# Merge gates of a hybrid encoder layer, computed two at a time as a block product of seven products in place of eight

## The chip, the cores and the metric

The kernel runs on one core of one Trainium2 chip. The metric is the time of the program on the device in microseconds. TensorE (PE) multiplies, its weight loads (PEld) run beside it; VectorE (DVE), ScalarE (ACT) and GpSimd (POOL) do the rest; SyncE (SP) issues DMAs.

## The reference, cut to what matters

Two layers. In each, x of 512 tokens by 1024 channels is projected once by w_in; the columns feed latent attention (branch A), differential attention (branch B) and the merge gates. All is float32.

```python
h = x @ w_in[l]
c_q, c_kv, k_r, gate_a, q_d, k_d, v_d, gate_b, gates = _split_cols(h)
...
y_a = o_a.transpose(0, 2, 1, 3).reshape(b, s, MLA_WIDTH) * jax.nn.silu(gate_a)
y_a = y_a @ w_branch_a[l]
...
y_b = o_b.transpose(0, 2, 1, 3).reshape(b, s, DIFF_WIDTH) * jax.nn.silu(gate_b)
y_b = y_b @ w_branch_b[l]
g = jax.nn.sigmoid(gates + b_merge[l])
merged = g[..., :D_MODEL] * y_a + g[..., D_MODEL:] * y_b
out = merged @ w_out[l]
x = _layer_norm(DEEPNORM_ALPHA * x + out, ln_gamma[l], ln_beta[l])
```

The gates are 2048 columns of w_in, sixteen blocks of 128 channels: eight for branch A (A0 to A7), eight for branch B.

## The kernel before, in words

**Number format.** Each float32 operand is held as two tiles, a rounded high part (written by ACT, a cast) and the rest (DVE, a subtraction), and each product is three matmuls: high by high, high by rest, rest by high (`mm3`, L123 to L126). x lies transposed in xH and xL, channels on the partitions in eight blocks (k), tokens along the free dimension.

**Weights.** `slot` (L107) loads a block of 128x1024 into a raw tile of tag wr (two buffers), casts it whole on ACT into a tile wh (L110), and subtracts in two halves on DVE into wl (L113); wh and wl have three buffers each. `proj` (L128) multiplies such a block with all of x: eight k by three matmuls of 128x512 into one bank of PSUM (tag acc, three buffers).

**Gates.** `gate` (L506) is one `proj` of block gtA c or gtB c and one tanh on ACT (L510); the sigmoid is (tanh + 1) / 2. `mergeA` (L514) multiplies it with the branch's product and keeps the result in SBUF (tag vs) until branch B's is added (L600, L601). `branch` (L496) multiplies the branch's output with w_branch, two blocks of 128 columns from one loaded slot (brA0 to brA3, brB0 to brB3).

**Order of work in a layer.** Latent projections; eight latent heads, of which the scores of one are woven with the values of the last; four differential heads, woven the same way; between them the lists `fill` and `dfill` put projections: g is a gate of branch A, m its merge, b, q, k, v are gate B, key, query and value projections. Branch B's gates and branches follow, then w_out and the normalisation. A scheduler then sets each engine's order from the program; each engine works in that order, and an instruction waits on the semaphores of what it reads or overwrites. A buffer of a tag is taken again in turn when its last reader is done. All loads are issued by SP, in one queue.

**Softmax.** `soft` (L167) takes a maximum on DVE and an exponential on ACT (L172) for each block of 128 queries; `keyT` (L175) transposes on PE and splits on ACT and DVE (L181, L182). `diff_k` (L411 on) splits a rotated key into four tiles: six casts on ACT (L413 to L420), two subtractions on DVE (L415, L416) after the rotation (L394 to L398).

GpSimd has only small powers (L236, L485, L645).

Of the kernel before, what the change touches and what calls it, by code (L numbers as in the profile page):

```python
# [50 lines left out]
def hybrid_trunk(ctx: ExitStack, tc: tile.TileContext, x, xT, wlat, wts, prm, dlam, gb, tab, rtab, out):  # L51
# [70 lines left out]

    def mm3(o, lh, ll, rh, rl, start, stop):  # L123
# [61 lines left out]
    def layer(l, last):  # L185
        pr = prms[:, l, :]
# [36 lines left out]
        for t in range(NT):  # L223
# [12 lines left out]
            nc.gpsimd.tensor_tensor(ss, ss, mhalf[:, 0:2], ALU.pow)  # L236
# [222 lines left out]
        def diff_values(h, pts, v, g, s1):  # L459
# [30 lines left out]
            yB.append(split(o, "lat"))  # L490
# [5 lines left out]
        def branch(which, c, ys):  # L496
# [3 lines left out]
            acc = pt_("acc")  # L500
# [5 lines left out]
        def gate(which, c):  # L506
            acc = proj(l, f"gt{'AB'[which]}{c}")
            th = t2("tmp")
            col = which * 8 + c
            nc.scalar.activation(th, acc, AF.Tanh, bias=bh[:, col:col + 1], scale=0.5)  # L510
# [27 lines left out]
        def run(names):  # L538
            for f in names:
# [3 lines left out]
                elif f[0] == "g":  # L543
                    hold[i] = gate(0, i)
# [238 lines left out]
```

## Time and profile before

| what | us |
|---|---|
| median of three runs (lowest, highest) | 858.61 (858.48, 859.12) |
| the profiled execution | 860.1 |
| its span in the trace | 858.3 |
| PE busy in it | 843.5 |
| DVE, ACT, POOL busy | 588.7, 429.0, 21.8 |
| bytes read from HBM, written | 70.80 MB, 4.19 MB |

A group's row reads: line, engine, operation, tile written <- tiles read, shapes, count; then busy us in all and mean ns of one; then how long the engine stood idle just before these and who ended it. A row of the timeline reads: start in us, length in us, engine, line, operation. Matmuls overlap each other, so their spacing is read from their starts. The granted clock of PE was 0.998 over the span.

### The profile page before, as it was taken

The page shows a single profiled execution, that of the slowest core. Times are in us where ns is not written, and L with a number is a line of the kernel's source. Part 1 is how long each engine was busy: PE and PEld are TensorE (multiplying, and loading weights), DVE is VectorE, ACT ScalarE, POOL GpSimd, SP SyncE. Part 2 cuts the span into 40 slices and gives each one's busy share as a digit, 9 for nine tenths or more (in the row PEclk, how much of TensorE's full clock was granted, in tenths as well). Part 3 has the DMA queues.
Part 4 walks back from the last instruction along what each step waited for, and adds up shares of the span by engine and source line. Part 5 has one row for each costly group of instructions (what it writes and reads, how often), then busy time and mean ns, then how long its engine had stood idle before and what let it go on. Part 6 is the DMA issues. An engine that isn't in the chain of part 4 may idle for free.

```text
span 858.3 us, 11026 instructions
## 1 busy us (share of the span) xinstructions
PE 843.5 (98%) x4121; PEld 693.1 (81%) x4121; DVE 588.7 (69%) x1066; ACT 429.0 (50%) x843; POOL 21.8 (3%) x30
## 2 busy tenths in 40 slices
PE   9899999999999999999999999999999999999996
PEld 7678778878888888888897878788788888888885
DVE  6789998686646745455857899876667466545457
ACT  5767786463534633332236776755546354433310
POOL 0100000000000000000110000000000000000001
PEclk9999999999999999999999999999999999999999
DMA  8310111213222352233514010112222223432322
GB/s 294 124 44 31 38 56 55 74 31 100 92 74 74 122 178 82 93 97 118 183 43 139 17 37 26 50 50 74 75 74 74 76 97 123 152 98 95 99 74 98
DMA packets 27701, 75.70 MB, mean 88 GB/s; under 512 B 3200, under 2 KB 7808, under 8 KB 27648
## 3 DMA queue, kind: packets, MB, share of 16 engines
q1 hardware_dynamic: 27648, 75.01, 27.4%
q8 instruction: 32, 0.52, 0.2%
q14 instruction: 21, 0.17, 0.1%
HBM read 70.80 MB, written 4.19 MB: 87 GB/s over the span
## 4 chain that ended last, share of the span: by engine, by line
PE 87%; ACT 5%; DVE 4%; DMA 2%; issue 1%; POOL 0%; SPq 0%; DVEq 0%; ACTq 0%
PE psacc L124 22%; PE psacc L126 22%; PE psacc L125 22%; PE pstr L179 4%; PE pspv L366 2%; PE pssc L124 2%; PE pspv L124 2%; PE pssc L126 2%; PE pssc L125 2%; PE pspv L367 1%; PE pspv L125 1%; PE pspv L126 1%; DMA wr<-in_wts_dram 1%; ACT wh L110 1%; PE pssc L445 1%; PE pssc L450 1%
## 5 line engine op out<-in xcount | busy, mean ns | idle before, releaser
L113 DVE TENSOR_TENSOR wl<-wr,wh 128x512 fp32r<-128x512 f32 x192 | 127.0, 687 | 149.4 <-ACT wh L110 149.0
L124 PE MATMUL psacc<-xH,wh 128*128 128x512 f32 x512 | 203.6, 398 | 0.0
L126 PE MATMUL psacc<-xH,wl 128*128 128x512 f32 x512 | 202.5, 395 | 0.0
L125 PE MATMUL psacc<-xL,wh 128*128 128x512 f32 x512 | 201.1, 393 | 0.0
L110 ACT CAST wh<-wr 128x1024 fp32r<-128x1024 f32 x96 | 100.6, 1049 | 177.2 <-PE psacc L125 111.8
L126 PEld LDWEIGHTS psacc<-xH,wl 128*128 128x128 f32 x512 | 96.4, 188 | 20.9
L125 PEld LDWEIGHTS psacc<-xL,wh 128*128 128x128 f32 x512 | 96.3, 188 | 20.4
L124 PEld LDWEIGHTS psacc<-xH,wh 128*128 128x128 f32 x512 | 96.4, 188 | 19.5
L172 ACT ACTIVATE p<-pssc,sm 128x512 f32<-128x512 f32 x128 | 88.1, 690 | 25.2 <-DVE sm L170 24.5
L170 DVE TENSOR_REDUCE sm<-pssc 128x1 f32<-128x512 f32 x128 | 86.8, 684 | 4.5 <-PE pssc L126 1.9
L182 DVE TENSOR_TENSOR pt<-pstr,pt 128x512 fp32r<-128x512 f32 x96 | 65.0, 686 | 8.4 <-ACT pt L181 7.8
L181 ACT CAST pt<-pstr 128x512 fp32r<-128x512 f32 x96 | 55.6, 586 | 27.7 <-PE pstr L179 27.2
L179 PE MATMUL pstr<-ident,p 128*128 128x128 f32 x384 | 57.3, 272 | 0.0
L179 PEld LDWEIGHTS pstr<-ident,p 128*128 128x128 f32 x384 | 47.4, 140 | 12.0 <-ACT p L172 0.5
L124 PE MATMUL psacc<-wh,xH 128*128 128x256 f32 (+1 forms) x164 | 48.8, 297 | 0.0
L125 PE MATMUL psacc<-wl,xH 128*128 128x256 f32 (+1 forms) x164 | 48.6, 296 | 0.1
L126 PE MATMUL psacc<-wh,xL 128*128 128x256 f32 (+1 forms) x164 | 48.0, 294 | 0.0
L125 PEld LDWEIGHTS psacc<-wl,xH 128*128 128x128 f32 x164 | 31.0, 189 | 1.2 <-DVE wl L203 0.8
L124 PEld LDWEIGHTS psacc<-wh,xH 128*128 128x128 f32 x164 | 30.8, 188 | 0.8 <-ACT xH L120 0.5
L126 PEld LDWEIGHTS psacc<-wh,xL 128*128 128x128 f32 x164 | 30.8, 188 | 0.2
L366 PE MATMUL pspv<-pt,vs 128*128 128x512 f32 x64 | 29.2, 456 | 0.6 <-ACT pt L181 0.3
L124 PE MATMUL pssc<-kv,qm 128*128 128x512 f32 x64 | 26.7, 422 | 0.4 <-ACT kv L323 0.2
(233 smaller groups left out, 1502.5 us busy)
## 6 DMA issues: line engine op xcount, KB each, us to landing
wr<-in_wts_dram SPq DMA_DIRECT2D x106, 512.0 KB, 3.6
p<-in_xT_dram SPq DMA_DIRECT2D x8, 256.0 KB, 5.2
qr<-in_wts_dram SPq DMA_DIRECT2D x16, 128.0 KB, 2.1
p<-in_gb_dram SPq DMA_DIRECT2D x8, 256.0 KB, 3.0
y<-in_x_dram SPq DMA_DIRECT2D x8, 256.0 KB, 4.8
x_scratch<-y SPq DMA_DIRECT2D x8, 256.0 KB, 2.1
y<-x_scratch SPq DMA_DIRECT2D x8, 256.0 KB, 5.2
out_dram<-y SPq DMA_DIRECT2D x8, 256.0 KB, 2.0
```

The lines of the kernel that those rows point to most:

```text
L110: nc.scalar.copy(hi, raw)
L113: nc.vector.tensor_tensor(lo[:, c], raw[:, c], fr(hi[:, c]), ALU.subtract)
L124: nc.tensor.matmul(o, lhsT=lh, rhs=rh, start=start, stop=False)
L125: nc.tensor.matmul(o, lhsT=lh, rhs=rl, start=False, stop=False)
L126: nc.tensor.matmul(o, lhsT=ll, rhs=rh, start=False, stop=stop)
L170: nc.vector.tensor_reduce(m, S, axis=AX.X, op=ALU.max, negate=True)
L172: nc.scalar.activation(p, S, AF.Exp, bias=m, scale=1.0, accum_out=sums)
L179: nc.tensor.transpose(b[:, t * P:(t + 1) * P], pts[t][:, c * P:(c + 1) * P], ident)
L181: nc.scalar.copy(h, b)
L182: nc.vector.tensor_tensor(lo, b, fr(h), ALU.subtract)
L366: nc.tensor.matmul(pv, lhsT=v, rhs=ph, start=kc == 0, stop=False)
L367: nc.tensor.matmul(pv, lhsT=v, rhs=pl, start=False, stop=kc == NT - 1)
```

## The change

**The scheme.** Two neighbouring gate blocks c and c + 1 are now one product. The weights are cut in four: rows by channel half (x blocks 0 to 3, or 4 to 7), columns by gate, called r11, r12, r21, r22 in the code; x is cut by channel half and by token half (256 tokens). Each quarter product is four k by three matmuls of 128x256. Seven are made in place of eight. Their weight sides are W11, W12, W22 and the sums F1, F2, F3, F4 of the raw quarters, made by four adds on POOL and each split on ACT and DVE like any weight (`form`); their x sides are blocks of xH and xL and four sums of x, `XF`.

**Sums of x.** `x_forms` makes them on POOL at the layer's start, behind the last small power there, 24 adds and subtractions, and stores them to DRAM by 8 DMAs that POOL issues. `load_x_form` loads them back by SP through tag wr behind the latent heads (x0, x1) and behind the first gate B projection (x2, x3), and splits them.

**Where the sums of products go.** Products share three banks: Y, Z and X, of tag acc. Y takes W11's, then is copied out and goes on accumulating F2's, F3's and W22's; Z takes F1's and F4's; X takes W12's. Copies and sums (on ACT and DVE, 256 columns each) give the two gates t0 and t1.

**Room.** Branch A's raw quarters take both buffers of tag wr; branch B's take four tiles of tag p. A pair takes four of the wh and wl buffers in turn: W11 and F1; F2 and F4; F3 and W12; W22. Branch B's products with w_branch go into tag sc.

**Branch A's half.** It is no longer kept in SBUF but stored to DRAM (`mAd`) and loaded back for branch B, both issued by POOL. yB's halves and the last two merged tiles take other tags. The packing puts two neighbouring gates' columns side by side; the time of that is not in the metric.

```diff
+        def x_forms(j):
+            ra, rb, f, g = (t2("y") for _ in range(4))
+            for r, k in ((ra, j), (rb, j + 4)):
+                nc.gpsimd.tensor_tensor(r, fr(xH[:, k, :]), fr(xL[:, k, :]), ALU.add)
+            c1, c2 = slice(0, 256), slice(256, 512)
+            nc.gpsimd.tensor_tensor(f[:, c1], ra[:, c1], ra[:, c2], ALU.subtract)
...
+            for i, v in ((0, f), (2, g)):
+                nc.gpsimd.dma_start(xf[:, i:i + 2, j * 256:(j + 1) * 256], v.rearrange("p (a b) -> p a b", a=2))
+        with tc.issue_after(last_pow.ins):
+            for j in range(4):
+                x_forms(j)
...
-            yB.append(split(o, "lat"))
+            yB.append(split(o, "qm" if h < 2 else "y"))
...
-            acc = pt_("acc")
+            acc = pt_("sc" if which else "acc")
...
-        def gate(which, c):
-            acc = proj(l, f"gt{'AB'[which]}{c}")
-            th = t2("tmp")
+        def gate_pair(which, c):
+            G = gates_of(l, which)[c // 2]
...
+            def form(raw, rm, half):
+                hi, lo = (v[:, half * 512:half * 512 + 512] for v in rm)
+                nc.scalar.copy(hi, raw)
+                nc.vector.tensor_tensor(lo, raw, fr(hi), ALU.subtract)
+                return hi, lo
+            def add(o, a, b):
+                nc.gpsimd.tensor_tensor(o, a, b, ALU.add)
+            r11, r12, r21, r22 = r
+            s1 = room()
+            W11 = form(r11, s1, 0)
+            add(r11, r11, r21)
+            add(r21, r21, r22)
+            F1 = form(r21, s1, 1)
+            add(r21, r11, r22)
+            s2, s3 = room(), room()
+            F2 = form(r21, s2, 0)
+            W12 = form(r12, s3, 1)
+            add(r12, r12, r21)
+            F4 = form(r12, s2, 1)
+            F3 = form(r11, s3, 0)
+            W22 = form(r22, room(), 0)
...
+            def product(o, w, xs_, first):
+                for k in range(4):
+                    (wh, wl), (h, lo) = (v[:, k * P:(k + 1) * P] for v in w), xs_[k]
+                    for n, (a, b) in enumerate(((wh, h), (wl, h), (wh, lo))):
+                        nc.tensor.matmul(o, lhsT=a, rhs=b, start=first and k == 0 and n == 0,
+                                         stop=k == 3 and n == 2, skip_group_check=True)
...
+            product(Y, W11, block(0, 0), True)
+            nc.scalar.copy(t0[:, c1], Y)
+            product(Z, F1, xform(0), True)
+            nc.scalar.copy(t1[:, c1], Z)
+            product(Y, F2, xform(1), False)
+            nc.scalar.copy(t0[:, c2], Y)
+            product(Z, F4, block(1, 1), False)
+            nc.vector.tensor_tensor(t0[:, c2], Z, t0[:, c2], ALU.add)
+            product(Y, F3, xform(2), False)
+            nc.scalar.copy(t1[:, c2], Y)
+            product(X, W12, block(1, 0), True)
...
+            product(Y, W22, xform(3), False)
...
-            m = mA[-1][:, (c % 2) * 512:(c % 2) * 512 + 512]
-            nc.vector.scalar_tensor_tensor(m, th, 1.0, acc, ALU.add, ALU.mult)
+            nc.vector.scalar_tensor_tensor(th, th, 1.0, acc, ALU.add, ALU.mult)
+            nc.gpsimd.dma_start(mAd[:, c * 512:(c + 1) * 512], th)
...
-        run(["b0", "v0"])
+        run(["b0", "x2", "x3", "v0"])
...
-            0: ["g0", "m0", "g1", "m1", "b1", "q2", "k2", "g2", "m2", "g3", "m3"],
-            1: ["v1", "b2", "q3", "k3", "g4", "m4", "g5", "m5"],
-            2: ["b3", "g6", "m6", "g7", "m7"],
+            0: ["b1", "p0", "m0", "m1", "q2", "k2", "p2", "m2", "m3"],
+            1: ["v1", "b2", "q3", "k3", "p4", "m4", "m5"],
+            2: ["b3", "p6", "m6", "m7"],
...
+                m = t2("kv")
+                nc.gpsimd.dma_start(m, mAd[:, c * 512:(c + 1) * 512])
```

**What stands where, first place: PE in layer 0, where head 2's scores follow branch A's second pair of blocks.** Before, the last matmuls of the branch (psacc_2315), then the scores of the key (qm_2213 to qm_2216), then transposes of head 1:

```order
L124 MATMUL psacc_2315<-y_1614,wh_2261 128x512
L125 MATMUL psacc_2315<-y_1615,wh_2261 128x512
L126 MATMUL psacc_2315<-y_1614,wl_2262 128x512
L445 MATMUL pssc_2330<-qm_2213,qm_2169 128x512
L446 MATMUL pssc_2330<-qm_2215,qm_2169 128x512
L449 MATMUL pssc_2337<-qm_2214,qm_2170 128x512
L450 MATMUL pssc_2337<-qm_2216,qm_2170 128x512
L179 MATMUL pstr_2349<-ident,p_1857 128x128
```

After, the last two matmuls of X (psacc_2395), the scores of the key (qm_2349 to qm_2352), then Z (psacc_2394, form F4 in wh_2374) and Y (psacc_2393, form F3 in wh_2376) by turns:

```order
L594 MATMUL psacc_2395<-xH,wl_2377 128x256
L594 MATMUL psacc_2395<-xL,wh_2376 128x256
L475 MATMUL pssc_2528<-qm_2349,qm_2305 128x512
L479 MATMUL pssc_2535<-qm_2350,qm_2306 128x512
L190 MATMUL pstr_2547<-ident,p_2031 128x128
L476 MATMUL pssc_2528<-qm_2351,qm_2305 128x512
L190 MATMUL pstr_2556<-ident,p_2031 128x128
L480 MATMUL pssc_2535<-qm_2352,qm_2306 128x512
L594 MATMUL psacc_2394<-xH,wh_2374 128x256
L594 MATMUL psacc_2393<-vs_1718,wh_2376 128x256
L594 MATMUL psacc_2393<-vs_1718,wl_2377 128x256
L594 MATMUL psacc_2394<-xH,wl_2375 128x256
```

Before, two gates and two branches stood between the key's projection and its scores; now the first four products of the pair stand there, and the scores stand inside the pair. The first matmuls of the branch (of weights wh_2492) stand now ahead of the pair's last product.

**Second place: ACT at the same point.** Before, behind the cast of gate A3's weights (wh_2283), the six casts of the key, then the tanh of gate A2:

```order
L110 CAST wh_2283<-wr_2281 128x1024
L413 CAST qm_2213<-tmp_2210 64x512
L414 CAST qm_2214<-tmp_2210 64x512
L418 CAST qm_2213<-qm_2213 64x512
L418 CAST qm_2215<-qm_2215 64x512
L420 CAST qm_2214<-qm_2214 64x512
L420 CAST qm_2216<-qm_2216 64x512
L510 ACTIVATE tmp_2257<-psacc_2232,bh_326 128x512
```

After, the key's six casts (L443 to L450), then form F4's (wh_2374), the copies of Z and Y, head 2's first exponentials, and the cast of the branch's weights (wh_2492), whose raw tile wr_2490 takes the buffer of wr_2361:

```order
L444 CAST qm_2350<-tmp_2346 64x512
L448 CAST qm_2349<-qm_2349 64x512
L450 CAST qm_2350<-qm_2350 64x512
L448 CAST qm_2351<-qm_2351 64x512
L450 CAST qm_2352<-qm_2352 64x512
L561 CAST wh_2374<-wr_2361 128x512
L604 COPY qw_2392<-psacc_2394 128x256
L606 COPY qw_2391<-psacc_2393 128x256
L183 ACTIVATE p_2533,s_469_1850<-pssc_2528,sm_2531 128x512
L192 CAST pt_2552<-pstr_2547 128x512
L183 ACTIVATE p_2540,sm_2527<-pssc_2535,sm_2538 128x512
L111 CAST wh_2492<-wr_2490 128x1024
```

F4's cast and the copies of the pair stand behind the key's casts, and the branch's cast behind them all.

**Third place: ACT in branch B, layer 0, third pair.** Before, casts of whole slots (L110), tanh (L510) and the split of merged tiles (L163):

```order
L110 CAST wh_3438<-wr_3436 128x1024
L510 ACTIVATE tmp_3355<-psacc_3330,bh_326 128x512
L110 CAST wh_3472<-wr_3470 128x1024
L510 ACTIVATE tmp_3389<-psacc_3364,bh_326 128x512
L163 ACTIVATE qm_3413<-tmp_3355 128x512
L110 CAST wh_3506<-wr_3504 128x1024
L163 ACTIVATE qm_3432<-tmp_3389 128x512
```

After, W12 and F3 (wh_3919), the copy of Y, F4 (wh_3917 from p_3901), a merged tile (qm_3896), W22 (wh_3930), the copies of Z and Y, the branch's weights (wh_4037):

```order
L561 CAST wh_3919<-p_3901 128x512
L561 CAST wh_3919<-p_3900 128x512
L602 COPY qw_3934<-psacc_3936 128x256
L561 CAST wh_3917<-p_3901 128x512
L174 ACTIVATE qm_3896<-tmp_3753 128x512
L561 CAST wh_3930<-p_3905 128x512
L604 COPY qw_3935<-psacc_3937 128x256
L606 COPY qw_3934<-psacc_3936 128x256
L111 CAST wh_4037<-wr_4035 128x1024
```

The copy of Z, which Z's second product waits for, stands behind F4's cast, a merged tile's and W22's.

More of the change, by code (lines that the diff above doesn't have):

```diff
@@ L39 @@
     + ["qd0", "kd0", "ga1", "qd1", "kd1", "ga2", "ga3"]
[3 rows of a table removed]
+    + ["vd00", "vd01", "gb0", "brA0", "gb1", "qd2", "kd2", "brA1"]
+    + ["vd10", "vd11", "gb2", "qd3", "kd3", "brA2", "gb3", "brA3"]
+    + ["brB0", "brB1", "brB2", "brB3"]
+    + [f"gt{w}{c}" for w in "AB" for c in range(8)]
     + [f"o{n}{k}" for n in range(2) for k in range(4)]
@@ L121, in load_x, with gates_of @@
         nc.vector.tensor_tensor(xL[:, k, :], raw, fr(xH[:, k, :]), ALU.subtract)
+    def gates_of(l, which):
+        i = SLOTS.index(f"gt{'AB'[which]}0")
+        return wts[l, i:i + 8].rearrange("(c s) (q r) n -> c (s q) (r n)", s=2, r=2)
     def mm3(o, lh, ll, rh, rl, start, stop):
@@ L185, in layer @@
     def layer(l, last):
+        xf = dram.tile([P, 4, 1024], F32, name=f"xf{l}")
+        mAd = dram.tile([P, 8 * 512], F32, name=f"mA{l}")
         pr = prms[:, l, :]
@@ L235, in layer @@
             nc.vector.tensor_scalar(ss[:, 1:2], ss[:, 1:2], 1.0 / 256, EPS_RMS, ALU.mult, ALU.add)
-            nc.gpsimd.tensor_tensor(ss, ss, mhalf[:, 0:2], ALU.pow)
+            last_pow = nc.gpsimd.tensor_tensor(ss, ss, mhalf[:, 0:2], ALU.pow)
             nc.vector.tensor_copy(kr[:, t, :], acc[:, 384:416])
@@ L542, in run @@
                     gateA(i)
-                elif f[0] == "g":
-                    hold[i] = gate(0, i)
+                elif f[0] == "p":
+                    hold[i], hold[i + 1] = gate_pair(0, i)
+                elif f[0] == "x":
+                    load_x_form(i)
                 elif f[0] == "m":
@@ L590, in layer @@
             run(dfill[h])
-        hold["B0"] = gate(1, 0)
+        ths = gate_pair(1, 0)
         next(tail)
@@ L594, in layer @@
         for c2 in range(4):
-            ths = [gate(1, 2 * c2) if c2 else hold.pop("B0"), gate(1, 2 * c2 + 1)]
+            if c2:
+                ths = gate_pair(1, 2 * c2)
             for i in range(2):
                 c = 2 * c2 + i
+                m = t2("kv")
+                nc.gpsimd.dma_start(m, mAd[:, c * 512:(c + 1) * 512])
                 acc = branch(1, c, yB)
@@ L600, in layer @@
                 nc.vector.scalar_tensor_tensor(th, th, 1.0, acc, ALU.add, ALU.mult)
-                nc.vector.tensor_tensor(th, th, mA[c // 2][:, i * 512:i * 512 + 512], ALU.add)
-                merged.append(split(th, "qm", 0.5))
+                nc.vector.tensor_tensor(th, th, m, ALU.add)
+                merged.append(split(th, "qm" if c < 6 else "pt", 0.5))
         src = x if l == 0 else xs
@@ L696, in _pack @@
         c = int(s[-1]) if s[-1].isdigit() else 0
+        if s.startswith("gt"):
+            if c % 2:
+                continue
+            o = O_GT + (DM if s[2] == "B" else 0) + c * P
+            a = np.concatenate([_fm(w_in, o + r(P)).reshape(P, DM), _fm(w_in, o + P + r(P)).reshape(P, DM)], 1)
+            outs += list(a.reshape(2, P, 1024))
+            continue
         if s.startswith("vd"):
@@ L701, in _pack @@
             a = _fm(w_in, o + c * P + r(P))
-        elif s.startswith("gt"):
-            a = _fm(w_in, O_GT + (DM if s[2] == "B" else 0) + c * P + r(P))
         elif s.startswith("qup"):
```

40 lines of the change are left out of this document (34 added, 6 removed), and 3 rows, old and new, of the table SLOTS.

## The prediction

> **What bounds the kernel now.** I read the page's first part, then the table of stretches over layer 0, then the groups by shape, then two timelines. The engine totals:
>
> ```profile
> PE 843.5 (98%) x4121; PEld 693.1 (81%) x4121; DVE 588.7 (69%) x1066; ACT 429.0 (50%) x843; POOL 21.8 (3%) x30
> ```
>
> The stretches of layer 0 in which the change acts (the columns are length, then busy time of PE, PEld, DVE, ACT and POOL, each with its instructions, then the granted clock, the DMA share and GB/s); they hold the differential heads with branch A's gates (172 to 300), and the last head and branch B (300 to 386):
>
> ```profile
> 172.00:300.00 128.00, 128.00 (x633) 105.76 (x632) 85.71 (x166) 65.14 (x139) 3.02 (x3) 1.00 0.26 82
> 300.00:327.00 27.00, 26.95 (x132) 21.77 (x131) 13.46 (x22) 10.65 (x22) 1.01 (x1) 1.00 0.45 148
> 327.00:386.00 59.00, 59.00 (x259) 48.41 (x258) 29.63 (x46) 20.73 (x26) 0.00 (x0) 1.00 0.31 97
> ```
>
> PE works 213.95 of these 214 us at full clock. So fewer PE cycles are worth their whole price here, and every wait that the change brings is paid in full as well: nothing is there to absorb it.
>
> **What the products take off PE.** Matmuls overlap, so their price is the step from one start to the next, not the duration in the third column. From PE's timeline, the first and last of 50 matmuls of 256 columns and of 67 of 512:
>
> ```profile
> 239.80 0.28 PE L125 MATMUL psacc<-wl,xH 128*128 128x256 f32 x1
> ...
> 245.57 0.28 PE L126 MATMUL psacc<-wh,xL 128*128 128x256 f32 x1
> 245.69 0.40 PE L124 MATMUL psacc<-xH,wh 128*128 128x512 f32 x1
> ...
> 261.09 0.40 PE L124 MATMUL psacc<-xH,wh 128*128 128x512 f32 x1
> ```
>
> 49 steps in 5.77 us are 0.118 us each; 66 steps in 15.40 us are 0.233. Half the columns cost half the time, weight loads included (they hide behind the matmuls in both). Before, 32 gates of 24 matmuls are 768 x 0.2333 = 179.2 us; after, 16 pairs of 84 are 1344 x 0.1178 = 158.3. That is 20.9 us less, 10.4 a layer, 1.3 a pair. One product is 12 x 0.118 = 1.41 us, a pair 9.9.
>
> **What must now be ready inside a pair.** A gate before had one cast, made long ahead, and one chain of 24 matmuls. A pair has seven forms, each an ACT cast and a DVE subtraction, four POOL adds between them, and copies of Y and Z that must be read out before PE goes on accumulating. The durations, from the groups:
>
> ```profile
> L113 DVE TENSOR_TENSOR wl<-wr,wh 128x512 fp32r<-128x512 f32 x192 | 127.0, 687 | 149.4 <-ACT wh L110 149.0
> L110 ACT CAST wh<-wr 128x1024 fp32r<-128x1024 f32 x96 | 100.6, 1049 | 177.2 <-PE psacc L125 111.8 <-issue 27.5 <-PE psacc L126 21.3
> L160 ACT CAST qm<-tmp 128x512 fp32r<-128x512 f32 x16 | 9.9, 619 | 3.5 <-DVE tmp L338 3.4
> L331 ACT CAST qw<-qr 128x256 fp32r<-128x256 f32 x16 | 6.5, 405 | 6.2 <-PE psacc L126 4.1 <-DMA qr<-in_wts_dram 1.3 <-PE pstr L179 0.7
> L394 DVE STREAM_SHUFFLE tmp<-psacc 128x512 f32<-128x512 f32 x16 | 11.9, 745 | 0.0
> wr<-in_wts_dram SPq DMA_DIRECT2D x106, 512.0 KB, 3.6
> ```
>
> So a half-width form is 0.62 us on ACT and 0.69 on DVE, a copy out 0.41, a load of weights 3.6. How soon another engine sees a product's end: the 256-wide chain above ended before 245.69, and ACT read it at 245.89, 0.2 us later:
>
> ```profile
> 245.89 0.59 ACT L160 CAST kv<-psacc 128x512 fp32r<-128x512 f32 x1 [0.32 <-PE psacc L126]
> ```
>
> **The POOL add is not in the trace.** Its bounds come from these rows:
>
> ```profile
> masks.py:199 POOL TENSOR_SCALAR_AFFINE_SELECT ident<-ident 128x128 f32<-128x128 f32 x1 | 0.3, 292 | 0.1
> L768 POOL MEMSET const-float32-0.0<- 128x1 f32 x1 | 0.1, 99 | 0.2 <-issue 0.2
> L645 POOL TENSOR_TENSOR sm<-sm,mhalf 128x1 f32<-128x1 f32 x8 | 7.4, 927 | 210.9 <-DVE sm L644 210.9
> L236 POOL TENSOR_TENSOR sm<-sm,mhalf 128x2 f32<-128x2 f32 x8 | 5.6, 705 | 39.0 <-DVE sm L235 25.3 <-DVE tmp L237 13.7
> ```
>
> The low end is DVE's own price for the same shape, 0.69. The select streams one input of 128 columns in 0.19 us over the memset's fixed 0.10, which makes 0.87 for 512 columns with one input; a second input may cost as much again, 1.64, the high end. With three streams (two read, one written) in place of the select's two it is 1.26. I take 1.2, between the select and that. The powers are no measure of it: a power of one column takes 0.93, of two 0.71. The Trainium skill ("GPSIMD Engine Reference", 3.1 Elementwise) gives about 2.6 cycles an element for this add, 4497 ns for 2048 columns; scaled, my estimate by that page is 1.12, no run here shows it yet, and the sum below would be 866.6 by it instead of 868.8.
>
> **Branch A, the two middle pairs of a layer (c = 2 and 4).** They follow the projection of a differential key, and the scheduler put that key's work ahead of form F4 on ACT and DVE. Let 0 be the end of the key's projection. At 0.2 DVE begins the shuffle, three products and sums and W12's subtraction: 0.75 + 4 x 0.69 = 3.5, so 3.7. Then ACT makes the key's six casts, which took 3.6 us before (211.98 to 215.59):
>
> ```profile
> 211.98 0.62 ACT L413 CAST qm<-tmp 64x512 fp32r<-64x512 f32 x1 [2.44 <-DVE tmp L398]
> 212.62 0.62 ACT L414 CAST qm<-tmp 64x512 fp32r<-64x512 f32 x1
> 213.26 1.14 ACT L418 CAST qm<-qm 64x512 fp32r<-64x512 f32 x2
> 214.43 1.14 ACT L420 CAST qm<-qm 64x512 fp32r<-64x512 f32 x2
> 215.59 0.69 ACT L510 ACTIVATE tmp<-psacc,bh 128x512 f32<-128x512 f32 x1
> ```
>
> They end at 7.3; only then come F4's cast (7.9), Z's copy (8.3) and Y's (8.7); F4's subtraction ends at 8.6. Only now is the raw tile with r12 free, and its buffer (there are two of tag wr) takes branch A's weights: a load of 3.6 and a cast of 1.05, so 13.25. PE could have been at the branch's first matmul at 9.8: four products 5.65, four score matmuls and two transposes 1.15, then Z and Y 2.8 and one value matmul 0.2. So it loses 3.4 us in each of these pairs, partly before Z and the rest before the branch, of which the POOL add is no part. Before, the same casts and the same load lay under gate and branch chains that stood there, which is why PE never paused. Two pairs: 6.8 us a layer.
>
> **Branch B, its last three pairs.** Only products and branches are left for PE: 9.9 + 24 x 0.233 = 15.5 us a pair. There are three buffers of weights, and a pair with its branch needs five, so W11's waits for the end of X of the pair before and W12's for the end of its branches. Let 0 be that end; X ended at -7.0 (Y 1.4, branches 5.6). W11: cast and subtraction done at -5.5. Two adds: -3.1. F1: -1.8. Third add: -0.5. F2's cast: 0.1. A cast of the merged tile (0.62) and W12's cast: 1.35. DVE has F2, the merged tile's rest and the merge of the second branch ahead of W12's subtraction: 2.75. Fourth add: 4.0. ACT then has, in this order, F4, a merged tile, W22 and at last Z's copy: three of 0.62 and one of 0.41, 6.2. PE wants to go on with Z at 4.2 after three products. The stall is 1.9 us, more than the pair's 1.3. By the same steps it is 0.1 with an add of 0.69 and 3.5 with 1.64, for all four adds are in one chain. Three pairs: 5.7 a layer (0.3 to 10.5).
>
> **The other pairs.** In A's first pair F1 and F2 stand on ACT ahead of exponentials that head 1's scores need: W11 can start only 1.4 us before the values' projection ends, two adds follow, and the exponentials come some 1.5 us late. In A's last pair the second raw tile is loaded after the branch's buffer is free, and the same happens to head 3's exponentials (1.4), with a Z copy behind F4 and W22 and a Y copy behind the branch's cast (0.9). In B's first pair the last head's split stands behind the next pair's F1 (1.2). Together 0 to 5.0; since each exponential may also be kept waiting by its own maximum, I take half, 2.5.
>
> **The rest.** The sums of x are 24 POOL adds and 8 stores a layer, begun when the last power is done; nobody reads them until the MLA heads end, some 100 us later. They run beside DVE work on which PE waits at a layer's start: 0 to 2 us, taken as 0.5. The four loaded forms add ACT casts of 1.05 and DVE work of 2 x 0.69 each, beside a stretch where PE was full and DVE busy 85.7 of 128 us: nothing, unless DVE is late, when it is within the half above. The 16 DMAs of branch A's halves a layer are issued by POOL and land long before they are read; one issue stands between the third and fourth add of B's second pair, at most one add, inside the range. Three halves of yB and two merged tiles change tags only; the loads of R behind the last branch have 22 us of the output's matmuls as cover.
>
> **The sum.** A layer: 6.8 + 5.7 + 2.5 + 0.5 - 10.4 = 5.1 us longer; two layers 10.2. The profiled execution took 860.1 (its span 858.3), 1.5 over the median of 858.61; the change is the same against both. The forecast is 868.8.
>
> **The rivals.**
> *The add is short (faster).* If POOL adds at DVE's price, 0.69, the place that decides is Z's copy in branch B: the stall there is 0.1, the other pairs lose some 0.8, x nothing, and a layer is 6.8 + 0.3 + 0.8 - 10.4 = -2.5: 853.6. It turns at an add of about 0.9 (0.8 x 3 + 1.2 + 6.8 = 10.4). For it: the select's 0.87. Against: that has one input. Chance 0.22.
> *No stall matters (faster).* Everything is ready as the order supposes: 858.6 - 20.9 = 837.7. For it: PE's 128.00 of 128 with much the same casts. Against: the six casts and the 3.6 us load, both measured. 0.07.
> *POOL and DVE hold each other up (slower still).* Nearly all of B's DVE work reads two SBUF tiles, and so does the add. If one must end before the other begins, each chained add waits half a DVE instruction more, 0.35: B's stall is 3.2, the other pairs pay 5.0, x 1.0, and a layer is 6.8 + 9.5 + 5.0 + 1.0 - 10.4 = 11.9 longer: 882.4. Both kinds in the trace of before:
>
> ```profile
> 847.15 1.41 DVE L648 SCALAR_TENSOR_TENSOR y<-y,sm,p 128x512 f32<-128x512 f32 x2
> 847.38 0.91 POOL L645 TENSOR_TENSOR sm<-sm,mhalf 128x1 f32<-128x1 f32 x1 [4.56 <-DVE sm L644]
> ```
>
> For it: beside DVE this power lasts 0.91, longer with one column than L236's with two. Against: it ended while DVE's second instruction still ran, and DVE's pair took no longer than two such instructions do. 0.20. The Trainium skill ("SBUF — State Buffer", Who interferes with whom) states this: a DVE instruction with two SBUF inputs contends with a GpSimd instruction that reads SBUF, and the second blocks; no run here shows it yet.
> *It cancels*, within 0.2% (what a measurement of this kernel can tell from no change): 0.06.
>
> **How the numbers follow.** The forecast has 0.45. Faster: 0.22 + 0.07 = 0.29; same 0.06; slower 0.45 + 0.20 = 0.65. With all high ends a layer is 6.8 + 10.5 + 5.0 + 2.0 - 10.4 = 13.9 longer, 886.4. The range goes from 850, just below the short add, to 886; outside lie the case without stalls and some of the last rival. The forecast's own case reaches from 863 to 876, an add of 1.0 to 1.4 (a layer 6.8 + 3.6 + 1.9 + 0.3 - 10.4 = 2.2, or 6.8 + 7.8 + 3.5 + 1.0 - 10.4 = 8.7, longer).
>
> **What would show it.** PE busy falls by about 21 us while its idle time grows from 15 to some 46. In A's middle pairs PE waits for the key's casts and F4 and then for the branch's cast, which waits for a DMA. In B the waits before Z's second product name ACT's copy or F4's subtraction, some 2 us, three times a layer. A POOL add of 512 columns lasts about 1.2 us. I am wrong if PE in branch B steps through a pair in under 11 us, or if the branch's weights in A come before PE does, or if the add is under 0.9; and in the other direction if DVE's 0.69 grows beside POOL.

## The result, and the profile after

| | us | ratio to before, 95% interval |
|---|---|---|
| before, median of 4 (lowest, highest) | 858.72 (858.48, 859.12) | |
| after, median of 4 (lowest, highest) | 931.43 (930.28, 933.80) | 1.085 (1.0828 to 1.0872) |
| the profiled execution's span, before and after | 858.3, 929.0 | |

The change made the kernel 8.5% slower; the forecast was 868.8, the range 850 to 886. The page of after, its engine totals:

```profile
PE 857.1 (92%) x4697; PEld 724.4 (78%) x4697; DVE 685.7 (74%) x1170; ACT 490.6 (53%) x1011; POOL 190.6 (21%) x190
```

PE was to be 21 us less busy and to idle some 46; it is 13.6 us more busy and idles 71.9 (929.0 less 857.1). The saving itself is there: a step of the new products, from one start to the next, takes 0.118 us in the median, as the prediction had it, and by count and price PE's steps sum to 20.9 us less than before. On top came waits, 74.1 us in steps more than 0.3 over their undisturbed price (7.3 before), and 24.4 us in steps that were less than 0.3 over it. The table of stretches shows both. Its columns are those of the prediction's table: length, busy time of PE, PEld, DVE, ACT and POOL, granted clock, DMA share and GB/s. It holds the layer's start, branch A's and branch B's pairs of layer 0, and three pairs of neighbouring stretches of 3.41 us:

```profile
28.00:38.00 10.00, 6.27 (x27) 4.91 (x26) 10.00 (x14) 3.32 (x7) 9.98 (x10) 0.88 0.20 66
161.85:165.26 3.41, 1.25 (x7) 0.83 (x7) 3.38 (x7) 1.42 (x3) 0.00 (x0) 1.00 0.51 154
165.26:168.67 3.41, 3.41 (x18) 3.41 (x17) 3.02 (x6) 1.87 (x4) 0.00 (x0) 0.50 0.44 161
172.00:300.00 128.00, 121.56 (x724) 104.44 (x723) 90.64 (x167) 70.52 (x152) 22.03 (x20) 0.99 0.26 81
233.53:236.94 3.41, 2.38 (x9) 1.21 (x9) 3.17 (x6) 2.92 (x7) 0.00 (x0) 1.00 0.45 154
236.94:240.35 3.41, 3.41 (x18) 3.41 (x17) 1.83 (x5) 2.20 (x6) 0.00 (x0) 0.50 0.51 154
288.14:291.55 3.41, 2.32 (x11) 1.23 (x10) 3.28 (x6) 2.90 (x5) 0.31 (x1) 1.00 0.23 52
291.55:294.97 3.42, 3.42 (x26) 3.08 (x26) 2.88 (x5) 3.30 (x10) 0.00 (x0) 1.00 0.48 151
327.00:408.00 81.00, 69.86 (x458) 62.99 (x458) 51.67 (x80) 39.46 (x82) 27.97 (x25) 0.98 0.39 128
```

The same ten microseconds of before, with the full clock and an idle POOL:

```profile
28.00:38.00 10.00, 10.00 (x51) 8.21 (x50) 8.27 (x17) 6.25 (x11) 0.00 (x0) 1.00 0.26 70
```

**Half clock.** In 165.26 to 168.67 PE is busy all the time and makes 18 matmuls at a granted clock of 0.50; in 291.55 to 294.97, as busy, 26 at 1.00. Twelve such half-clock stretches lie between the start and the end of after (two of them adjoin), none in before. Their starts stand on a fixed grid: 35.55 and 165.26 are 129.71 apart, 38 times 3.4133. If one counts on that grid how long PE idled (steps beyond their price, because the modelled ends in the busy column overlap), the stretches just ahead of half clock idled 2.02 to 3.41 us (2.69 from 161.85, 2.19 from 233.53), and no other more than 1.98 (that from 288.14). At half clock a step of 512 columns takes 0.427 us in place of 0.233 and one of 256 takes 0.213 in place of 0.118, so a stretch that is full of work costs 1.5 us. (The expectations below reckon with 1.7, half of the stretch.) Over all twelve, some of them partly idle, this is 14.7 of the 24.4 us. The other 9.7 are steps at full clock, each less than 0.3 us over its price; what delayed these was not followed.

**GpSimd and VectorE.** The groups by shape:

```profile
L114 DVE TENSOR_TENSOR wl<-wr,wh 128x512 fp32r<-128x512 f32 x128 | 97.3, 789 | 39.2 <-ACT wh L111 39.2
L181 DVE TENSOR_REDUCE sm<-pssc 128x1 f32<-128x512 f32 x128 | 86.8, 682 | 5.6 <-PE pssc L137 2.4 <-PE pssc L476 2.0 <-PE pssc L480 0.7
L566 POOL TENSOR_TENSOR p<-p,p 128x512 f32<-128x512 f32 x32 | 45.1, 1410 | 87.7 <-DVE wl L562 72.9 <-issue 14.2
L317 POOL TENSOR_TENSOR y<-xH,xL 128x512 f32<-128x512 f32 x16 | 21.9, 1373 | 0.1
L566 POOL TENSOR_TENSOR wr<-wr 128x512 f32<-128x512 f32 x8 | 10.3, 1286 | 0.6
```

The maximum before:

```profile
L170 DVE TENSOR_REDUCE sm<-pssc 128x1 f32<-128x512 f32 x128 | 86.8, 684 | 4.5 <-PE pssc L126 1.9 <-PE pssc L450 1.2 <-PE pssc L446 0.4
```

The subtraction that had 687 ns now has 789 in the mean; the maximum, whose input lies in PSUM, has 682 where it had 684. Of the 128 subtractions 116 had no GpSimd add beside them and took 684, twelve had one for over 30% of their time and took 1039 to 2502. The timeline of the layer's start, POOL and DVE alone, shows how:

```profile
28.83 1.39 POOL L317 TENSOR_TENSOR y<-xH,xL 128x512 f32<-128x512 f32 x1
28.97 1.34 DVE L290 TENSOR_TENSOR tmp<-tmp,p 128x64 f32<-128x64 f32 x1
...
30.82 0.21 DVE L291 TENSOR_TENSOR tmp<-tmp,p 128x64 f32<-128x64 f32 x1
...
32.72 1.31 POOL L317 TENSOR_TENSOR y<-xH,xL 128x512 f32<-128x512 f32 x1
32.83 1.48 DVE L362 TENSOR_TENSOR qw<-qr,qw 128x256 fp32r<-128x256 f32 x1
...
35.36 3.48 DVE L114 TENSOR_TENSOR wl<-wr,wh 128x512 fp32r<-128x512 f32 x2
36.48 1.82 POOL L317 TENSOR_TENSOR y<-xH,xL 128x512 f32<-128x512 f32 x1
```

L290 and L291 are the same operation on the same shape: 1.34 us when it began just after an add, and it ended 0.1 us after the add; 0.21 when it began 0.1 us before the end of an add of 256 columns. The two engines exclude each other on such instructions. The Trainium skill (SBUF — State Buffer, Who interferes with whom) says so: an exclusive lock, the later one blocks. These rows agree.

**PE's waits**, in us in all, times, longest:

```profile
PE psacc L594 <- ACT tmp L604: 8.8, 4, 2.7
PE pssc L475 <- ACT p L183: 8.7, 5, 2.7
PE psacc L594 <- ACT qw L604: 5.8, 3, 2.7
PE psacc L135 <- DVE g L160: 5.7, 2, 4.3
PE pstr L297 <- DVE tmp L294: 5.2, 2, 3.7
PE psacc L136 <- DVE wl L114: 3.7, 2, 1.8
```

L604 is Z's copy, as forecast for branch B. L183 is a head's exponential. The last three are the layers' starts (g and tmp), where the sums of x run, and the first differential values, whose weights (L114) now come behind the loaded forms x2 and x3.

One of branch B's pairs on POOL, ACT and DVE, from its first add to Z's copy:

```profile
376.16 2.65 POOL L566 TENSOR_TENSOR p<-p,p 128x512 f32<-128x512 f32 x2 [8.22 <-DVE wl L562]
378.84 0.62 ACT L561 CAST wh<-p 128x512 fp32r<-128x512 f32 x1 [2.17 <-POOL p L566]
379.50 0.69 DVE L562 TENSOR_TENSOR wl<-p,wh 128x512 fp32r<-128x512 f32 x1 [3.43 <-ACT wh L561]
...
380.27 1.29 POOL L566 TENSOR_TENSOR p<-p,p 128x512 f32<-128x512 f32 x1 [1.46 <-DVE wl L562]
380.82 1.29 DVE L710 TENSOR_TENSOR tmp<-tmp,kv 128x512 f32<-128x512 f32 x1
...
384.88 1.60 POOL L566 TENSOR_TENSOR p<-p,p 128x512 f32<-128x512 f32 x1 [3.32 <-issue]
...
386.51 0.62 ACT L561 CAST wh<-p 128x512 fp32r<-128x512 f32 x1 [2.44 <-POOL p L566]
387.04 0.62 ACT L174 ACTIVATE qm<-tmp 128x512 fp32r<-128x512 f32 x1
387.57 0.60 ACT L561 CAST wh<-p 128x512 fp32r<-128x512 f32 x1
388.08 0.36 ACT L604 COPY qw<-psacc 128x256 f32<-128x256 f32 x1
```

The chain of the prediction is there link by link: two adds, F1, an add, F2 and W12, the fourth add, F4, a merged tile, W22, Z's copy. From the first add to the copy's start it takes 11.9 us; the prediction's steps make that 11.3. In this chain the lock costs only the fourth add's 0.3 (1.60 for 1.29).

In branch A's second pair it shows too. Beside the fourth add (230.67, 1.61 us) the first of two subtractions took 1.79 us and not 0.69; the key's own subtractions stood behind them, one of its casts waited 0.36 us for these, and PE for that cast. The rows show also when the branch's weights were loaded (SP) and cast (L111), and when F4 was cast (L561) and its rest taken (L562):

```profile
231.04 2.39 DVE L562 TENSOR_TENSOR wl<-wr,wh 128x512 fp32r<-128x512 f32 x2
233.49 0.33 SPq L105 DMA_DIRECT2D wr<-in_wts_dram  x1
235.42 0.62 ACT L561 CAST wh<-wr 128x512 fp32r<-128x512 f32 x1
236.07 0.69 DVE L562 TENSOR_TENSOR wl<-wr,wh 128x512 fp32r<-128x512 f32 x1
239.64 1.05 ACT L111 CAST wh<-wr 128x1024 fp32r<-128x1024 f32 x1
```

### The profile page after: what moved, and what is told of

It is laid out like the page before. It is cut to its first block, busy times and chain, and to the rows that moved or that the text cites. A ratio compares the mean times of both kernels' runs of the same rounds, so it can differ in the third digit from the quotient of the medians.

```text
span 929.0 us, 12866 instructions
## 1 busy us (share of the span) xinstructions
PE 857.1 (92%) x4697; PEld 724.4 (78%) x4697; DVE 685.7 (74%) x1170; ACT 490.6 (53%) x1011; POOL 190.6 (21%) x190
## 3 DMA queue, kind: packets, MB, share of 16 engines
q1 hardware_dynamic: 31104, 79.20, 26.5%
## 5 line engine op out<-in xcount | busy, mean ns | idle before, releaser
L114 DVE TENSOR_TENSOR wl<-wr,wh 128x512 fp32r<-128x512 f32 x128 | 97.3, 789 | 39.2 <-ACT wh L111 39.2
L135 PE MATMUL psacc<-xH,wh 128*128 128x512 f32 x256 | 102.8, 402 | 0.0
L137 PE MATMUL psacc<-xH,wl 128*128 128x512 f32 x256 | 101.8, 398 | 0.0
L111 ACT CAST wh<-wr 128x1024 fp32r<-128x1024 f32 x64 | 67.0, 1048 | 65.5 <-DMA wr<-in_wts_dram 32.9
L136 PE MATMUL psacc<-xL,wh 128*128 128x512 f32 x256 | 101.3, 396 | 0.0
L183 ACT ACTIVATE p<-pssc,sm 128x512 f32<-128x512 f32 x128 | 88.3, 692 | 22.7 <-DVE sm L181 21.8
L562 DVE TENSOR_TENSOR wl<-wr,wh 128x512 fp32r<-128x512 f32 x56 | 44.0, 795 | 41.3 <-ACT wh L561 40.1
L561 ACT CAST wh<-wr 128x512 fp32r<-128x512 f32 x56 | 34.1, 619 | 71.9 <-POOL wr L566 45.8
L594 PE MATMUL psacc<-xH,wh 128*128 128x256 f32 x192 | 57.2, 298 | 14.8 <-ACT tmp L604 8.8
L562 DVE TENSOR_TENSOR wl<-p,wh 128x512 fp32r<-128x512 f32 x56 | 42.5, 765 | 35.6 <-ACT wh L561 34.6
L566 POOL TENSOR_TENSOR p<-p,p 128x512 f32<-128x512 f32 x32 | 45.1, 1410 | 87.7 <-DVE wl L562 72.9
L561 ACT CAST wh<-p 128x512 fp32r<-128x512 f32 x56 | 33.7, 615 | 55.4 <-POOL p L566 52.0
L137 PEld LDWEIGHTS psacc<-xH,wl 128*128 128x128 f32 x256 | 48.6, 190 | 10.1
L594 PE MATMUL psacc<-vs,wh 128*128 128x256 f32 x256 | 55.7, 299 | 0.7 <-ACT qw L610 0.7
L136 PEld LDWEIGHTS psacc<-xL,wh 128*128 128x128 f32 x256 | 48.6, 190 | 9.7
L594 PE MATMUL psacc<-xH,wl 128*128 128x256 f32 x192 | 55.8, 291 | 0.3
```

The source lines that it names most:

```text
L111: nc.scalar.copy(hi, raw)
L114: nc.vector.tensor_tensor(lo[:, c], raw[:, c], fr(hi[:, c]), ALU.subtract)
L135: nc.tensor.matmul(o, lhsT=lh, rhs=rh, start=start, stop=False)
L136: nc.tensor.matmul(o, lhsT=lh, rhs=rl, start=False, stop=False)
L137: nc.tensor.matmul(o, lhsT=ll, rhs=rh, start=False, stop=stop)
L183: nc.scalar.activation(p, S, AF.Exp, bias=m, scale=1.0, accum_out=sums)
```

## The experiments

The kernel before was run beside each set on the same chip (858.78, 860.53, 858.37 and 858.94 us), so sets are compared by their ratios. After's is 1.085.

| run | us | ratio (95%) |
|---|---|---|
| e1_no_xsums | 912.53 | 1.0622 (1.0600 to 1.0643) |
| e2_no_wsums | 875.15 | 1.0190 (1.0175 to 1.0205) |
| e3_wsums_dve | 894.14 | 1.0413 (1.0396 to 1.0431) |
| e4_clock | 892.96 | 1.0398 (1.0377 to 1.0419) |
| e5_xsums_later | 921.19 | 1.0717 (1.0671 to 1.0763) |
| e6_v0_first | 927.38 | 1.0794 (1.0773 to 1.0815) |
| e7_three_edits | 875.49 | 1.0182 (1.0149 to 1.0215) |
| e8_branch_after_key | 870.32 | 1.0119 (1.0103 to 1.0135) |
| e9_paced | 886.79 | 1.0337 (1.0320 to 1.0355) |
| e10_pairs_in_B | 875.77 | 1.0204 (1.0189 to 1.0220) |
| e11_B_xsums_dve | 857.18 | 0.9979 (0.9970 to 0.9988) |
| e12_B_wsums_pool | 883.99 | 1.0287 (1.0271 to 1.0303) |

**The sums of x.**

```diff
-        with tc.issue_after(last_pow.ins):
-            for j in range(4):
-                x_forms(j)
-            XF.append(split(load(xf[:, i, :]), tag, -1.0 if i == 1 else None))
+            XF.append(split(load(xT[:, i * 1024:(i + 1) * 1024]), tag, -1.0 if i == 1 else None))
```

> The sums of x are left out: GpSimd neither adds nor stores them, and the four loaded forms are read from the transposed input in DRAM instead, the same bytes. Theory: beside these adds VectorE's work at the layer's start is held up, TensorE idles there 10.6 and 10.2 us instead of 3.4 and 3.3, and three stretches of 3.41 us at half clock follow (1.7 us each). Without them the time falls by 14 + 5 = 19 us, to about 912, and VectorE's 1.48 and 3.5 us rows at 32 to 44 us are gone. Rival (the step of the prediction): the sums cost at most 2 us a layer, so 927 to 931, and TensorE's waits at the start stay.

The time is 912.5, as the theory had it. The ten microseconds at the layer's start are those of before again, though x's forms are still loaded and split:

```profile
28.00:38.00 10.00, 10.00 (x52) 8.19 (x51) 8.41 (x20) 6.98 (x13) 0.00 (x0) 1.00 0.23 66
```

So the sums of x cost 19 us, though nobody reads them for another 100 us.

**The sums of weights.** First e2, then e3:

```diff
             def add(o, a, b):
-                nc.gpsimd.tensor_tensor(o, a, b, ALU.add)
+                pass
```

```diff
             def add(o, a, b):
-                nc.gpsimd.tensor_tensor(o, a, b, ALU.add)
+                nc.vector.tensor_tensor(o, a, b, ALU.add)
```

> The four adds of weights in each gate pair are left out; the seven forms are cast from the raw quarters. Everything else is as after. Theory: in branch B the chain of four adds (1.35 us each) is what makes form F4, and so Z's copy behind it on ScalarE, late; without it the waits before Z's second product (2.0 to 2.9 us, three a layer) go, those of A's middle pairs shrink, and with them five or six stretches at half clock: 2 x (7.5 + 2) + 6 x 1.7 = 29 us less, about 902. Rival: the copies are late by ScalarE's own order (casts of F4, merged tile and W22 ahead of Z's copy), adds or none; then the waits in B stay above 1.5 us and the time is 920 or more.

> The four adds of weights in each gate pair are made by VectorE instead of GpSimd; the sums of x stay on GpSimd. Theory: an add takes 0.69 instead of 1.35 us and nothing is held up by a second engine, so the wait before Z's second product in B falls from 2.0 to 2.9 us to under 1, and most half-clock stretches in the pairs go: 912 to 918. Rival: VectorE is the scarce engine there; 64 adds a run of 0.69 us are 44 us more of it, its subtractions and merges come later, and the time stays at 925 to 940.

Without the adds 875, with VectorE's 894, both below their forecasts. Both rivals fall, and the theory was too timid: all of branch A's waits for exponentials but 0.7 and all for key casts went with the adds as well. A cast on ACT that waits for an add holds up everything behind it in ACT's order. So the four adds a pair cost 56 us on POOL and 19 on DVE. With VectorE's no wait on L604 is left; the longest in the pairs is now for a form in branch A:

```profile
PE psacc L594 <- ACT wh L561: 4.9, 4, 2.5
PE pssc L475 <- ACT p L183: 3.7, 4, 1.9
```

**The clock by itself**, on the kernel before:

```diff
                 merged.append(split(th, "qm", 0.5))
+                if c < 7:
+                    d, e = pt_("sc"), t2("op")
+                    nc.scalar.copy(e[:, 0:P], acc[:, 0:P])
+                    for _ in range(2 * c + l):
+                        nc.gpsimd.tensor_copy(e[:, 0:P], e[:, 0:P])
+                    nc.tensor.transpose(d[:, 0:P], e[:, 0:P], ident)
```

> The kernel before, with a wait of TensorE made on purpose after each of the first seven branches of B: a corner of the branch's result is copied to SBUF, GpSimd copies it in place 2c times in layer 0 and 2c+1 times in layer 1 (c is the branch), and TensorE transposes it into a bank that nobody reads. So TensorE idles for fourteen spells from about 0.5 to some 4 us. Theory, from the trace after (every stretch of its clock's 3.41 us grid in which TensorE idled 2.0 us or more was followed by a stretch at half clock, no other was): spells of 2 us that lie within one stretch bring half clock, spells under 2 do not, and each such stretch costs 1.7 us on top of the wait. Rival: only a stretch that is idle from end to end, 3.41 us, does it (the half clocks after were due to something else in the change); then only the longest two or three spells are followed by half clock, if any. The Trainium skill (TensorE: Matmul & The Clock Gate, What's actually happening) states the rival's rule: half rate after at least one idle window of some 3.4 us.

The waits were up to 3.9 us. Stretches of its own grid, which half clock shows to start at 396.11:

```profile
368.81:372.22 3.41, 2.56 (x12) 1.76 (x10) 2.64 (x5) 2.13 (x4) 2.31 (x7) 1.00 0.48 154
372.22:375.63 3.41, 2.07 (x10) 1.73 (x11) 2.52 (x4) 0.63 (x2) 3.13 (x6) 1.00 0.26 24
...
795.46:798.88 3.42, 1.36 (x7) 0.80 (x7) 1.24 (x2) 0.00 (x0) 2.15 (x6) 1.00 0.53 133
798.88:802.29 3.41, 3.41 (x10) 2.67 (x9) 0.00 (x0) 0.00 (x0) 0.00 (x0) 0.50 0.05 20
```

A wait of 2.2 us inside the stretch from 795.46 brought half clock; one of 2.3 at 371.2, which the grid cut into 1.0 and 1.3, did not. Four stretches idled 2.17 to 3.22 us and were followed by half clock; the others idled at most 2.00 and were not. In the other runs the boundary, among stretches at full clock, lies at 2.0 us as well, within 0.1 by how the smallest delays are counted. The theory holds, but for the price: the four stretches cost 5.8 us, 1.45 each, and not 1.7. The Trainium skill (TensorE: Matmul & The Clock Gate, What's actually happening) states the window's length of 3413 ns and that it runs freely, and these grids agree; its condition, an idle window, is too strict here if a wholly idle one is meant, for 2.17 us of 3.41 were enough.

**Later sums, earlier values.** First e5, behind the loop that makes VS, then e6:

```diff
-        with tc.issue_after(last_pow.ins):
+        mark = nc.gpsimd.tensor_copy(small(1), fr(VS[3])[:, 0:1])
+        with tc.issue_after(mark.ins):
             for j in range(4):
                 x_forms(j)
```

```diff
-        run(["b0", "x2", "x3", "v0"])
+        run(["b0", "v0"])
-            0: ["b1", "p0", "m0", "m1", "q2", "k2", "p2", "m2", "m3"],
+            0: ["b1", "x2", "x3", "p0", "m0", "m1", "q2", "k2", "p2", "m2", "m3"],
```

> All of the change, but GpSimd begins the sums of x some 20 us later: behind a copy of one column of the last value tile of the MLA stage, so that they run beside the MLA heads. Theory (GpSimd's adds and VectorE's instructions with two SBUF inputs exclude each other): in the MLA stage most VectorE work has an input in PSUM, which the trace after shows unharmed beside the adds (0.68 us), so the loss at the layer's start goes, waits and three half-clock stretches, and at most 4 us come back in queries: 912 to 917. Rival: wherever they stand, 40 us of sums a layer hold VectorE up, which is busy 90.5 of 102 us in that stage; then 924 or more.

> All of the change, but the two forms x2 and x3 are loaded after the weights of the first differential values instead of ahead of them, just before the first pair. Theory: the waits of 0.48 and 2.00 us at 161.7 us (and the same at 621.5) and the half-clock stretch behind each go: 2 x (2.4 + 1.7) = 8 us less, 923. Rival: the wait only moves, to the first pair, which needs both forms 20 us later: 929 to 935.

By the ratios e5 gains 11 us and e6 5, each between theory and rival. In e5 the starts are better, but a new wait of 3.4 us stands at 56 us, where a VectorE split behind adds is late for the first head's values. (e5's executions spread from 917.6 to 927.4 us, and the profile is of the one of 927.4.) In e6 the values' wait is gone (its row has left the list), and the next exponential, at 174 us, is 0.9 us later than in after, 2.7 in place of 1.75. A part of each loss only moves.

**All three, and a new order in branch A.** e7 joins e3, e5 and e6; e8 also puts key and query between a pair and its branches:

```diff
-            0: ["b1", "x2", "x3", "p0", "m0", "m1", "q2", "k2", "p2", "m2", "m3"],
-            1: ["v1", "b2", "q3", "k3", "p4", "m4", "m5"],
-            2: ["b3", "p6", "m6", "m7"],
+            0: ["b1", "x2", "x3", "p0", "q2", "k2", "m0", "m1", "p2"],
+            1: ["v1", "b2", "q3", "k3", "m2", "m3", "p4"],
+            2: ["b3", "m4", "m5", "p6", "m6", "m7"],
```

> Three edits together: sums of x beside the MLA heads, values' weights ahead of x2 and x3, sums of weights on VectorE. Theory: the three losses are separate, so the savings add: 894 with the weights' sums on VectorE, less 15 to 19 at the layer's start, less 8 for the loads: 867 to 871. Rival: the same time is saved twice, or VectorE becomes the bound: 880 or more.

> The three edits, and in branch A the order is pair, differential query and key, then the pair's two branches, instead of pair, branches, query and key: the branches' 5.6 us stand between a key's casts and the next pair, as gates and branches did in the kernel before. Theory: the waits for late forms in A's middle pairs (2.6 + 0.9 + 0.8 and 2.2 + 0.9 + 1.6 us with VectorE's sums) and two half-clock stretches go: 12 us less than with the three edits, 855 to 859, about the kernel before. Rival: the waits are those of the heads' exponentials behind casts on ScalarE and only move: the same as with the three edits, within 3 us.

The ratios are 1.018 and 1.012. e7 misses its upper bound by 4.5 us because e5 and e6 had saved less than forecast: singly the three edits save 37.5, 11.4 and 4.8 us by the ratios, 53.7 in all, and together 57.4, so the savings do add. e8 gains 5 us and not 12. Its longest wait is again the one that the sums of x cause beside the first heads:

```profile
PE pspv L398 <- DVE pt L193: 5.4, 2, 3.2
```

The split that these values wait for stood behind this subtraction on VectorE:

```profile
55.60 4.26 DVE L363 TENSOR_TENSOR qw<-qr,qw 128x256 fp32r<-128x256 f32 x1
```

It takes 0.41 us undisturbed. It began with the first of five sums of x that followed each other on GpSimd from 55.58 to 59.57, and ended 0.3 us after the last. So the two engines do not alternate: an instruction of VectorE can wait for a whole row of GpSimd's.

**Spread sums**, in wh and wl tiles (e9), and with them pairs in branch B alone, A's `gate` and packing as before (e10):

```diff
+            def op(t, o, a, b, alu):
+                mark = nc.gpsimd.tensor_copy(small(1, "mk", 2), pts[t][:, 0:1])
+                with tc.issue_after(mark.ins):
+                    nc.gpsimd.tensor_tensor(o, a, b, alu)
...
+            if h < 4:
+                x_forms(h, ps_[h + 1])
```

```diff
-            2: ["b3", "m4", "m5", "p6", "m6", "m7"],
+            0: ["g0", "m0", "g1", "m1", "b1", "q2", "k2", "g2", "m2", "g3", "m3"],
+            1: ["v1", "b2", "q3", "k3", "g4", "m4", "g5", "m5", "x0", "x1"],
+            2: ["b3", "g6", "m6", "g7", "m7", "x2", "x3"],
```

> As with the branches behind the key (sums of weights on VectorE, values' weights first), but the sums of x are spread over the MLA heads 0 to 3, a GpSimd add behind a copy of one column of each score tile, in spare weight buffers. Theory: adds that follow one another leave VectorE no gap, so that one of its instructions waits for several of them (3.4 us of TensorE's wait at 57 us and 2.4 at 502 us, and half clock behind); with a gap after each, VectorE waits at most for one. 5 to 8 us less than with the sums in one piece, 862 to 865. Rival: what counts is the sum of the overlap, not its order; then the same loss is spread over the heads, within 2 us of 870.

> Pairs in branch B alone, with VectorE's sums of weights and the spread sums of x; branch A's gates are made as before the change, and the four forms of x are loaded in the second half of branch A. Theory: in B nothing waits once the sums of weights are VectorE's, so half of the 20.9 us is kept whole, less at most 4 for the sums of x: 852 to 856 where the kernel before takes 859 to 861. Rival: the loads and casts of the four forms, now beside differential heads and gates, make the exponentials late there as the pairs did; then 859 or more.

Both forecasts fall: 1.034 is worse than e8's 1.012, and e10 is at 1.020. In both the new waits stand in heads 0 to 3; in e10 nothing waits behind them, neither in A nor in B, so its number fits the rival but not the rival's reason. The longest wait, 3.8 us in each layer of both, is again for a head's split. It is not the lock's. In e10, the split and GpSimd's next instruction:

```profile
71.23 1.28 DVE L193 TENSOR_TENSOR pt<-pstr,pt 128x512 fp32r<-128x512 f32 x2
72.19 0.18 POOL L320 COPY mk<-p 128x1 f32<-128x1 f32 x1 [8.35 <-ACT p L183]
```

GpSimd stands idle for 8.35 us up to 72.19, and the eleven VectorE instructions that run there ahead of the split take 0.67 to 0.73 us each, their usual time. The scheduler has put a differential query's rotation and splits ahead of the head's split. Over the whole run, what VectorE's instructions took beyond the usual time of their shape sums to some 4 us in e9 and e10 and to some 11 in e8. So the gaps did what they were to do, and the new order on VectorE made the longest wait; why the scheduler chose that order, and the shorter waits for exponentials, were not followed.

**No sums on GpSimd.** e11 has pairs in B, weights' sums on VectorE, and x's too, in groups of six behind gates of A (0, 2, 4 and 5); e12 is e11 with the weights' sums back on POOL.

```diff
+            with tc.issue_after(mark[0].ins):
                 for r, k in ((ra, j), (rb, j + 4)):
-                    nc.gpsimd.tensor_tensor(r, fr(xH[:, k, :]), fr(xL[:, k, :]), ALU.add)
+                    nc.vector.tensor_tensor(r, fr(xH[:, k, :]), fr(xL[:, k, :]), ALU.add)
```

> Pairs in branch B alone, and GpSimd adds nothing: the sums of weights are VectorE's, and so are the sums of x, four groups of six behind gates of branch A, whose gates are made as before the change. Theory: with no engine holding VectorE up and no pair beside a head's key or exponentials, TensorE waits no more than before the change, and half of the 20.9 us is kept, less up to 3 for groups of 3 us on VectorE: 848 to 852 where the kernel before takes 858.6. Rival: VectorE's 24 sums a layer make the heads late in branch A, 0.5 us or more for each group, and the forms' casts as well: 855 or more.

> The same, but the sums of weights in branch B's pairs are GpSimd's, as in the change. Theory: B's waits come back as they were in the change (1.8 and 1.7 us around the first pair, 2.0, 2.9 and 2.5 before the second products of the others, in each layer) with three or four stretches at half clock: 2 x 11 + 4 x 1.7, some 25 to 29 us more than with VectorE's sums. Rival: those waits came from what the change had done ahead of B (late yB, POOL's stores, forms); then less than 15 us more.

e11, half of the change, is 0.2% faster than the kernel before: 857.18 (11 runs) against 858.94. That is above its forecast of 848 to 852 and in the rival's range. Its longest waits are old ones at a layer's start:

```profile
PE pstr L259 <- ACT qm L252: 2.5, 4, 1.3
PE psacc L136 <- DVE vs L345: 2.3, 2, 1.2
```

In the profiled runs its products save 10.5 us of steps as they should; waits give 3.0 back and slightly longer steps 3.6. Of the 3.0, two waits for exponentials in branch A (0.87 us at 281 and 1.11 at 703) make 2.0, as the rival had it but only once a layer; the cause of the longer steps was not followed. e12 adds 26.5 by the ratios, within its 25 to 29, with the waits on Z's copy at after's sizes (2.0, 2.8, 2.5) though branch A is undisturbed, and five stretches at half clock:

```profile
PE psacc L595 <- ACT tmp L605: 8.8, 4, 2.7
PE psacc L595 <- ACT qw L605: 5.4, 2, 2.7
```

## Why the prediction was wrong in size

The direction and the mechanism in branch B were right. What failed are three terms that the prediction put at nothing or near it: the sums of x beside VectorE's work at the layer's start (1.0 us a run, measured 14.5 in waits), the loaded forms ahead of the values (0, measured 5.0), and the clock (no term, measured 14.7). The waits in the pairs were also set too low, at 30.0 for 46.8. The sum, in us a run, by PE's steps of the two profiles:

| term | forecast | measured |
|---|---|---|
| products | -20.8 | -20.9 |
| waits in pairs, A | +17.4 | +23.4 |
| waits in pairs, B | +12.6 | +23.4 |
| layer's start (sums of x) | +1.0 | +14.5 |
| forms ahead of the values | 0 | +5.0 |
| steps at half clock | 0 | +14.7 |
| other steps less than 0.3 over their price | 0 | +9.7 |
| elsewhere | 0 | +0.9 |
| sum | +10.2 | +70.7 |

(The 2.5 a layer of the "other pairs" is split 1.9 to A and 0.6 to B.)

- **"What the products take off PE"**: right. The -20.9 is the trace's count at the same price; what confirms it is the step of 0.118 us.
- **The add, "I take 1.2"**: right; 1.29 where nothing is beside it.
- **"Branch B, its last three pairs"**: right in its chain, 2.0 to 2.9 us for 1.9 (its own 6.2 less 4.2 is 2.0). B's first pair was too small: 1.8, 0.3 and 1.7 for 1.2, by an exponential's split and y's split behind forms that wait for adds.
- **"Branch A, the two middle pairs"**: half right. PE waited for the key's casts and Z's copy, but not for the branch's weights. The step that failed is the buffer: their raw tile does not take the place of the one with r12, which F4 is cast from, but of the other, with r21 and r22 (the text ahead of the prediction names the wrong one too). So their load left at 233.49, when W22's subtraction ended, while F4's cast began only at 235.42; their cast was done at 240.7, 0.5 us before PE, itself late, needed them. The two pairs cost 5.8 us a layer for 6.8. The last pair's exponential waited 2.9 and 2.0 us, not the 1.4 allowed.
- **"The rest ... 0 to 2 us, taken as 0.5"** failed: e1 shows 19 us a run, half clock included. The prediction had the lock as a rival, with the right rule, but gave x 1.0 a layer even there. An isolated add delays a VectorE instruction once; 24 in a row leave it hardly a gap (4.26 us for 0.41 in e8), and that stretch of VectorE's work is what PE waits for.
- **"The four loaded forms ...: nothing, unless DVE is late"** failed: 2.5 us a layer, and half clock behind each.
- **No term for the clock.** The prediction priced a wait at its length. A wait that puts 2.0 us or more of idleness into one grid stretch costs up to 1.5 us more; with waits of 2 us and more spread over the kernel, twelve stretches were at half clock.

What stays open is how the lock and POOL's length share the 56 us of the weights' adds (in branch B's chain above the lock is 0.3 of 11.9 us, in branch A's second pair it lengthened a subtraction by 1.1; the other pairs were not followed), and what makes up the 9.7 us of small delays.

## What to carry to other kernels

Before work is moved to GpSimd, list the VectorE instructions with two SBUF inputs beside it, and count each as waiting for the add; in a row, count all of the row. Price a wait of TensorE of about 2 us and more at its length plus a half-clock stretch, 1.5 us here, unless the grid cuts it. Behind an in-order engine's wait for a slow neighbour stands everything else of that engine: here the exponentials.

## What the runs showed of the hardware that was not expected

Half clock does not need an idle stretch of the whole 3.41 us: with 2.17 us it came, in e4, and with 2.00 it did not. Half clock costs less than half of the stretch, 1.5 of 3.41 us, because a step of 512 columns grows from 0.233 to 0.427 us and not to twice its length. Whether a wait of 2.0 to 3.4 us triggers it depends on where the grid cuts it. In e4, GpSimd's copies of 128x128 (one input) took 0.29 us where VectorE began behind them and 0.63 when a VectorE instruction with two SBUF inputs had begun first; beside them VectorE's subtraction took 0.77 in place of 0.69. So an instruction with one SBUF input on GpSimd takes part in the lock as well. Beside VectorE's instructions with one input in PSUM (L600) the copies kept their 0.29. And GpSimd's instructions in a row can keep VectorE out through all of them: 4.26 us in e8 for a subtraction of 0.41.
